# Hybrid RWKV-7 / S5 layer on one core: gelu of the S5 results in fill work, stored in channel order; a tanh behind the sines; the second half's natural layout behind the first half's outputs

## The chip, the cores and the metric

The kernel runs on one core of a Trainium2 chip. Its time is the device time of one execution in microseconds (us), and the time of a kernel is the median over its runs. Next to the times there is one profiled execution, of which a trace shows every instruction of the engines: TensorE (PE, matrix products), VectorE (DVE), ScalarE (ACT), GpSimd (POOL) and SyncE (SP, which here only issues DMA transfers).

## The reference

One decoder layer over 1024 tokens with 1024 channels, fp32. The parts that matter:

```python
h = rms_norm(x, norm_mix_pre)
proj = h @ w_in                      # RWKV inputs | S5 input u (512) | two gates (2 x 1024)
gates = jax.nn.sigmoid(proj[..., N_RWKV_COLS + S5_WIDTH:] + b_gate)
o_rwkv = rwkv7_branch(p_rwkv, ...) @ w_branch_rwkv
# s5_branch: y = Re(C states) + d * u per group of 16 channels, then
y = jax.nn.gelu(y)
o_s5 = (y * jax.nn.sigmoid(y @ w_glu + b_glu)) @ w_branch_s5
mixed = (g_rwkv * o_rwkv + g_s5 * o_s5) @ w_out
x = x + rms_norm(mixed, norm_mix_post)
h = rms_norm(x, norm_ffn_pre)
x = x + rms_norm(conv_ffn(h, ...), norm_ffn_post)
```

`rwkv7_branch` is a recurrence over the tokens with a 64x64 state for each of 8 heads; S5 is a diagonal complex recurrence.

## The kernel before

Every large fp32 product is made of three matmuls on operands split into a high and a low part: L172 (high by high), L173 (low by high) and L174 (high by low). A tile is 128 channels by 512 tokens, so the 1024 tokens are two halves, th = 0 and 1. Matmuls of 512 columns start every 0.227 us at full clock.

The work runs in stages. To about 270 us: input norm, the S5 input projection and the S5 scan in four batches, whose tables come from Sin (L573, L574). Each batch leaves its results in HBM in `YU` (L616), in the scan's layout. Then, for each half, the RWKV stages run as lanes of generators:

- the **front** (`rwkv_front`, for two groups g of two channel tiles u): loads of k, v, r and others from `RKV`, `TZ`, `TA` (L652); Square of k on ACT (L667); Exp (L673, L674); column sums `st` on PE into PSUM buffers `rp` (L681); their inverse roots on DVE and back into `yb` on ACT (L687); transposes `kb` (L701); then the grams (L715, the four-part products inside a chunk);
- the **natural layout** (`rwkv_nat`, L741 for keys, `nat_v` L756 for values): PE transposes that ACT copies out (L748, L750, L761);
- the **inversion** (`rwkv_inv`): a transpose on DVE (L784) of what ACT copies into it (L773), 31 steps of two DVE operations each (L795, L797), a transpose back (L798);
- the **level** (`rwkv_level`): transposes on DVE (L812), small products on PE (L822 and after);
- the **chain** over the chunks (`rwkv_chain`), and the **output** (`rwkv_out`): norm on DVE, PE transposes (L935), ACT evictions (L937), loads of `bv` and `TG` (L944), stores to `YR` (L950).

The chain of half 0 runs at about 392 to 453 us, that of half 1 at about 600 to 700 us.

Beside these lanes lies the **fill** work, a list of generators that yield one small block of matmuls at a time: `gate_tiles` (the 16 tiles of gate projections, evicted by a Tanh on ACT, L1158, and stored to `GT`, L1159), `merge` (`gate` L1203, `glu_tile` L1187, L1188; it loads `YR` at L1210 and the S5 results by `s5_y`), later the output projection. `s5_y` loads a strided piece of `YU` (L1177) and applies gelu on ACT (L1178), which also puts it into channel order. A planner gives each lane's step a latency (T_ numbers, us), and places fill blocks until the step is due; that sets the order of PE, which runs its instructions as written. The other engines' orders follow from a scheduler with priorities. All loads and stores of this region are issued by SP, one after the other: an issue that waits holds the ones behind it.

PSUM buffers: `gm` (products of fill) has two, `rp` two, `cz` two per pair. In SBUF the pool `ld` has ten tiles, the weights' pools four.

Of the kernel before, what the change touches and what calls it, by code (L numbers as in the profile page):

```python
# [66 lines left out]
class Kern:  # L67
# [425 lines left out]
    def s5_tables(self, b, d):  # L493
# [78 lines left out]
        A.activation(cs, ph, AF.Abs)  # L572
        A.activation(sn, ph, AF.Sin, scale=SIN_SCALE)  # L573
        A.activation(cs, cs, AF.Sin, bias=self.hpi, scale=-SIN_SCALE)  # L574
        A.copy(ph, s["rho"][:, g8].unsqueeze(2).to_broadcast([128, 8, 128]))
        G.memset(ph[:, :, 0:1], 0.0)

# [220 lines left out]
            V.transpose(mt.rearrange("p (e t) -> p t e", t=32), x.rearrange("p (q t) -> p t q", t=32))  # L798
            self.diagonal(ds, mt, True)

    def rwkv_level(self, ds):

        A, V = self.nc.scalar, self.nc.vector
        mm = self.nc.tensor.matmul
        lo, hi = (slice(0, 32), slice(64, 96)), (slice(32, 64), slice(96, 128))
        tie = self.rp((128, 8, 64))
        self.nat_v(ds[1], 1, tie)
        Z = [self.tg("ld", NLD).rearrange("p (u c t) -> p u c t", u=2, t=32) for _ in ds]
        for d, xz in zip(ds, Z):
            A.copy(xz[:, :, 0, 0:1], tie[:, 0:2, 0:1])  # L810
            for h in range(2):
                V.transpose(xz[lo[h]].rearrange("p u c t -> p (u c) t"),  # L812
                            d["gr"][lo[h], :, :, h, 0:32].rearrange("p u c t -> p (u c) t"))
        P = [[x.rearrange("p (k c t) -> p k c t", k=2, t=32) for x in y] for y in (self.cz(), (self.rp(), self.rp()))]
        yield 0.4, T_LT
        self.chain_v(ds, 0)
        kw = dict(stop=True, skip_group_check=True)
        for d, p, xz in zip(ds, P, Z):
            for u in range(2):
                for c in range(8):  # L820
                    for h in range(2):
                        mm(p[u][hi[h], 0, c], d["gr"][lo[h], u, c, h, 32:64], xz[lo[h], u, c], start=c == 0, **kw)  # L822
        for p, xz in zip(P, Z):
            for u in range(2):
                for h in range(2):
                    A.copy(xz[hi[h], u], p[u][hi[h], 0])
        yield 1.6, T_LV
        for d, p, xz in zip(ds, P, Z):
            for u in range(2):
                for c in range(8):  # L830
                    for h in range(2):
                        mm(p[u][lo[h], 1, c], xz[hi[h], u, c], d["gr"][hi[h], u, c, h, 32:64], start=c == 0, **kw)
        for d, p in zip(ds, P):
            for u in range(2):
                for h in range(2):
                    A.copy(d["gr"][lo[h], u, :, h, 32:64], p[u][lo[h], 1])
        yield 1.6, T_LV
# [334 lines left out]
    def lx(self):  # L1172
        return self.lxp.tile([128, 512], F32R, tag="lx", name=self.nm("lx"))

    def s5_y(self, t, b, th, y):

        self.nc.sync.dma_start(t, self.YU[b].rearrange("j c g n -> (c g) j n")[:, :, th * 64:th * 64 + 64])  # L1177
        self.nc.scalar.activation(y.rearrange("p (n j) -> p j n", j=8), t, AF.Gelu_apprx_tanh)  # L1178
        return y

    def glu_tile(self, m, xs, t, y, br, to):
# [34 lines left out]
    def merge(self, mg):  # L1216
# [8 lines left out]
            self.split(*br[k], self.yr[k])  # L1225
        xs, ys = [], []

        def inputs(bs):
            for b in bs:
                y = self.hp[0].tile([128, 512], F32, tag=f"hh{4 + b}", name=self.nm("hh"), bufs=1)  # L1230
                ys.append(self.s5_y(self.tg("ld", NLD, (128, 8, 64)), b, 0, y))
                xs.append(self.pair(1, 4 + b))
                self.split(*xs[b], y)
        yield 0
        first = []
        for i in range(NK + MGAP):
# [18 lines left out]
    def s5_inputs(self, b):  # L1255

        assert self.fronts == 4
        self.ys5.append(self.s5_y(self.ev((128, 8, 64)), b, 1, self.tg("ld", NLD)))
        self.xs5.append(self.pair(0, b))
        self.split(*self.xs5[b], self.ys5[b])  # L1260

# [478 lines left out]
    def build(self):  # L1740
        tc, nc = self.tc, self.nc
        with tc.tile_pool(name="const", bufs=1) as self.const, tc.tile_pool(name="small", bufs=1) as self.small, \
# [7 lines left out]

            self.US = [dr(f"US{m}", (8, 16, 8, 128)) for m in range(4)]
            self.YU = [dr(f"YU{m}", (8, 16, 8, 128)) for m in range(4)]
            self.YR = [dr(f"YR{m}", (128, 512)) for m in range(4)]
            self.X1 = dr("X1", (D, T))
            self.H0 = [dr(f"H0{k}", (128, 512)) for k in range(NK)]
# [60 lines left out]
    def front_half(self):  # L1816
# [8 lines left out]
        with tc.tile_pool(name="lxp", bufs=4) as self.lxp, tc.tile_pool(name="s5c", bufs=1) as self.s5c, \  # L1825
# [4 lines left out]
            with tc.tile_pool(name="xp", bufs=1) as xp:  # L1830
                with tc.high_priority(HPN):
                    self.setup(xp)
                    self.s5w = {}
                    self.start(xp)
                    self.setup_vecs()
                with tc.high_priority(HP):
                    self.s5_setup()
                self.fill = [self.mix_in()] + [self.gate_tiles(m) for m in range(14)] + [
                    self.merge_loads(), self.gate_tiles(14, 15)]
                self.outs, self.yr = 0, []  # L1840
            with tc.tile_pool(name="s5p", bufs=1) as self.s5p:
                self.s5d = [{} for _ in range(4)]
# [45 lines left out]
    def chain_lane(self):  # L1888
        for th in range(2):
            ds = self.ds[th]  # L1890
            yield 0, lambda: self.fronts >= 2 * th + 1
            self.rwkv_nat(ds[0], 0)
            yield 2.0, (lambda: self.preps > th), 2.5
            yield from self.rwkv_level(ds)
            yield 0, lambda: self.outs >= 2 * th
            yield from self.rwkv_chain(ds, self.pts[th], th)
            if th:
# [17 lines left out]


T_US, T_TAB0, T_TAB, T_TRIG, T_SCAN = 5.0, 44.0, 20.0, 12.0, 24.0
T_LD, T_SQ, T_LT = 6.0, 3.0, 3.5
NEVA = 4
T_KN, T_BK, T_GR, T_NF, T_MT, T_INV, T_LV, T_CH = 7.0, 4.0, 4.0, 5.0, 3.0, 34.0, 1.0, 0.8  # L1920
T_LN, T_LE, T_INV2 = 32.0, 16.0, 46.0
# [4 lines left out]
NLD = 10  # L1926
# [80 lines left out]
```

## Time and profile before

| what | value |
|---|---|
| median of 3 runs | 1463.06 us (1462.29 to 1465.25) |
| profiled execution, its own time | 1461.26 us |
| its span | 1459.5 us |
| mean granted TensorE clock | 0.986 |

A row of the timeline gives start and duration in us, engine, line and operation, output and input by name, and in brackets how long the engine had been idle and what ended it. A row of the waits gives who waited for whom: us in total, times, longest. A row of the windows gives the busy time (and number of instructions) of PE, PE's weight loads, DVE, ACT and POOL, the granted TensorE clock, the busy share of the DMA engines and GB/s. An arrow as in `ld<-YU` reads "ld is written from YU".

### The profile page before, as it was taken

The page shows a single profiled execution, that of the slowest core. Times are in us where ns is not written, and L with a number is a line of the kernel's source. Part 1 is how long each engine was busy: PE and PEld are TensorE (multiplying, and loading weights), DVE is VectorE, ACT ScalarE, POOL GpSimd, SP SyncE. Part 2 cuts the span into 40 slices and gives each one's busy share as a digit, 9 for nine tenths or more (in the row PEclk, how much of TensorE's full clock was granted, in tenths as well). Part 3 has the DMA queues.
Part 4 walks back from the last instruction along what each step waited for, and adds up shares of the span by engine and source line. Part 5 has one row for each costly group of instructions (what it writes and reads, how often), then busy time and mean ns, then how long its engine had stood idle before and what let it go on. Part 6 is the DMA issues. An engine that isn't in the chain of part 4 may idle for free. (4 is left out here: it accounts for less than half of the span.)

```text
span 1459.5 us, 23887 instructions
## 1 busy us (share of the span) xinstructions
PE 1402.2 (96%) x9156; PEld 1142.9 (78%) x9156; DVE 1087.5 (75%) x1783; ACT 746.7 (51%) x1197; POOL 34.9 (2%) x80
## 2 busy tenths in 40 slices
PE   7999999999999989899999999999999999999996
PEld 5778888878878767678788887888888887888785
DVE  8986886378327788548688898777777777597677
ACT  7667775453424564535455464454544445444451
POOL 0000000000000000000000000000000000000001
PEclk9999999999999999899999999999999999999998
DMA  7454433542413565433555543222222228934723
GB/s 221 116 190 128 144 117 108 188 146 80 139 60 110 162 193 165 138 111 116 172 195 180 158 133 122 87 83 76 75 84 87 87 73 273 328 112 144 239 79 115
DMA packets 119682, 202.04 MB, mean 138 GB/s; under 512 B 28672, under 2 KB 34944, under 8 KB 119568
## 3 DMA queue, kind: packets, MB, share of 16 engines
q1 hardware_dynamic: 113296, 182.43, 39.4%
q0 software_dynamic: 4544, 15.80, 2.9%
q10 hardware_dynamic: 1728, 2.29, 0.4%
q8 instruction: 72, 1.18, 0.3%
q14 instruction: 42, 0.34, 0.1%
HBM read 148.04 MB, written 50.33 MB: 136 GB/s over the span
## 5 line engine op out<-in xcount | busy, mean ns | idle before, releaser
L172 PE MATMUL gm<-hh,wh 128*128 128x512 f32 x672 | 276.2, 411 | 9.1 <-DVE hl L1203 4.6
L173 PE MATMUL gm<-hl,wh 128*128 128x512 f32 x672 | 264.8, 394 | 0.0
L174 PE MATMUL gm<-hh,wl 128*128 128x512 f32 x672 | 264.6, 394 | 0.0
L156 ACT CAST wh<-wf 128x512 fp32r<-128x512 f32 x171 | 105.2, 618 | 140.9 <-PE gm L173 72.5
L157 DVE TENSOR_TENSOR wl<-wf,wh 128x512 fp32r<-128x512 f32 x171 | 117.2, 688 | 76.2 <-ACT wh L156 75.6
L172 PEld LDWEIGHTS gm<-hh,wh 128*128 128x128 f32 x672 | 127.5, 190 | 41.5 <-DVE hl L1203 5.7
L174 PEld LDWEIGHTS gm<-hh,wl 128*128 128x128 f32 x672 | 127.7, 190 | 27.8
L173 PEld LDWEIGHTS gm<-hl,wh 128*128 128x128 f32 x672 | 127.8, 190 | 24.7 <-issue 1.0
L1626 PE MATMUL d<-xl,wh 128*128 128x512 f32 x308 | 120.7, 392 | 2.1 <-DVE xl L227 2.0
L1625 PE MATMUL d<-xh,wh 128*128 128x512 f32 x308 | 120.8, 392 | 2.1 <-ACT xh L226 2.1
L1627 PE MATMUL d<-xh,wl 128*128 128x512 f32 x308 | 120.6, 392 | 0.0
L1451 PE MATMUL rp<-t,h 128*128 128x512 f32 x216 | 84.4, 391 | 1.5 <-ACT p L1465 1.5
L1453 PE MATMUL rp<-t,l 128*128 128x512 f32 x216 | 84.2, 390 | 0.5 <-DVE l L227 0.5
L1452 PE MATMUL rp<-t,h 128*128 128x512 f32 x216 | 84.1, 389 | 0.0
L1626 PEld LDWEIGHTS d<-xl,wh 128*128 128x128 f32 x308 | 58.2, 189 | 15.5 <-DVE xl L227 3.4
L1625 PEld LDWEIGHTS d<-xh,wh 128*128 128x128 f32 x308 | 58.2, 189 | 14.6 <-ACT xh L226 2.4
L1627 PEld LDWEIGHTS d<-xh,wl 128*128 128x128 f32 x308 | 58.1, 189 | 12.0
L226 ACT CAST h<-r 128x1024 fp32r<-128x1024 f32 x34 | 35.8, 1054 | 61.1 <-PE rp L1452 29.6
L227 DVE TENSOR_TENSOR l<-r,h 128x1024 fp32r<-128x1024 f32 x34 | 41.6, 1225 | 29.2 <-ACT h L226 27.7
L1472 DVE SCALAR_TENSOR_TENSOR y<-zv,vecs,y 128x1023 f32<-128x1023 f32 (+1 forms) x36 | 46.1, 1281 | 8.5 <-ACT y L1470 8.5
L1465 ACT COPY p<-rp 128x512 f32<-128x512 f32 x54 | 31.0, 574 | 36.6 <-PE rp L1453 36.6
L1451 PEld LDWEIGHTS rp<-t,h 128*128 128x128 f32 x216 | 40.5, 188 | 11.1 <-ACT p L1465 2.4
(459 smaller groups left out, 3127.6 us busy)
## 6 DMA issues: line engine op xcount, KB each, us to landing
r<-in_w_up_dram SPq DMA_DIRECT2D x36, 512.0 KB, 3.6
wf<-in_w_in_dram SPq DMA_DIRECT2D x62, 256.0 KB, 3.0
st<-in_w_down_dram SPq DMA_DIRECT2D x55, 256.0 KB, 4.0
st<-ACT SPq DMA_DIRECT2D x44, 256.0 KB, 4.3
wf<-in_w_up_dram SPq DMA_DIRECT2D x36, 256.0 KB, 2.9
ACT<-y POOLq DMA_DIRECT2D x18, 512.0 KB, 2.9
GT<-ev SPq DMA_DIRECT2D x32, 256.0 KB, 2.5
wf<-in_w_br_dram SPq DMA_DIRECT2D x32, 256.0 KB, 2.6
```

What stands on the lines that cost most here:

```text
L156: nc.scalar.copy(h[:, :n], f[:, :n])
L157: nc.vector.tensor_tensor(l[:, :n], f[:, :n], h[:, :n].bitcast(F32), ALU.subtract)
L172: mm(ps, a, xh[k], start=k == 0, stop=False)
L173: mm(ps, a, xl[k], start=False, stop=False)
L174: mm(ps, b, xh[k], start=False, stop=k == n - 1)
L1451: mm(ps, wh[:, c], xh, start=first and k == 0, stop=False, skip_group_check=True)
L1452: mm(ps, wh[:, c], xl, start=False, stop=False, skip_group_check=True)
L1453: mm(ps, wl[:, c], xh, start=False, stop=k == 3, skip_group_check=True)
L1472: V.scalar_tensor_tensor(y[:, lag:], z[:, 0:1024 - lag], self.vec(nme, i), y[:, lag:], ALU.mult, ALU.add)
L1625: mm(ps, wh[:, c], xh[:, x], start=start, stop=False, skip_group_check=True)
L1626: mm(ps, wh[:, c], xl[:, x], start=False, stop=False, skip_group_check=True)
L1627: mm(ps, wl[:, c], xh[:, x], start=False, stop=stop, skip_group_check=True)
```

## The change

Four edits. (a) `s5_tables` of the last batch ends with a Tanh of one column, so that ACT's table is changed behind the last Sin and not at the first gate tile. (b) A new piece of fill work, `s5_ready`, loads a piece of `YU`, applies gelu and stores it to new tensors `Y5` in HBM in channel order; eight of them stand behind the gate tiles 6 to 13. `s5_y` is then one contiguous load of `Y5`. `merge` issues its four loads at its start, into the tiles `hh4` to `hh7`. (c) `chain_lane` places the natural layout of the second half behind the outputs of the first. (d) The latency of the level is 6.0 instead of 3.5 us for the second half, which puts nine more fill matmuls in front of its products.

```diff
@@ s5_tables
         A.activation(cs, cs, AF.Sin, bias=self.hpi, scale=-SIN_SCALE)
+        if b == 3:
+            A.activation(self.edge[:, 0:1], cs[:, 0, 0:1], AF.Tanh)
@@ rwkv_level
-    def rwkv_level(self, ds):
+    def rwkv_level(self, ds, latency):
...
-        yield 0.4, T_LT
+        yield 0.4, latency
@@ s5_y
-    def s5_y(self, t, b, th, y):
-
+    def s5_ready(self, b, th):
+
+        t, y = self.tg("ld", NLD, (128, 8, 64)), self.tg("ld", NLD)
         self.nc.sync.dma_start(t, self.YU[b].rearrange("j c g n -> (c g) j n")[:, :, th * 64:th * 64 + 64])
         self.nc.scalar.activation(y.rearrange("p (n j) -> p j n", j=8), t, AF.Gelu_apprx_tanh)
+        self.nc.sync.dma_start(self.Y5[b][:, th * 512:th * 512 + 512], y)
+        yield 0
+
+    def s5_y(self, b, th, y):
+
+        self.nc.sync.dma_start(y, self.Y5[b][:, th * 512:th * 512 + 512])
         return y
@@ merge
+        for b in range(4):
+            y = self.hp[0].tile([128, 512], F32, tag=f"hh{4 + b}", name=self.nm("hh"), bufs=1)
+            ys.append(self.s5_y(b, 0, y))
+
         def inputs(bs):
             for b in bs:
-                y = self.hp[0].tile([128, 512], F32, tag=f"hh{4 + b}", name=self.nm("hh"), bufs=1)
-                ys.append(self.s5_y(self.tg("ld", NLD, (128, 8, 64)), b, 0, y))
                 xs.append(self.pair(1, 4 + b))
-                self.split(*xs[b], y)
+                self.split(*xs[b], ys[b])
@@ s5_inputs
-        self.ys5.append(self.s5_y(self.ev((128, 8, 64)), b, 1, self.tg("ld", NLD)))
+        self.ys5.append(self.s5_y(b, 1, self.tg("ld", NLD)))
@@ the tensors in HBM
+            self.Y5 = [dr(f"Y5{m}") for m in range(4)]
@@ the list of fill work
-                self.fill = [self.mix_in()] + [self.gate_tiles(m) for m in range(14)] + [
-                    self.merge_loads(), self.gate_tiles(14, 15)]
+                self.fill = [self.mix_in()] + [self.gate_tiles(m) for m in range(6)]
+                for i in range(8):
+                    self.fill += [self.gate_tiles(6 + i), self.s5_ready(i % 4, i // 4)]
+                self.fill += [self.merge_loads(), self.gate_tiles(14, 15)]
@@ chain_lane
-            yield 0, lambda: self.fronts >= 2 * th + 1
+            yield 0, lambda: self.fronts >= 2 * th + 1 and self.outs >= 2 * th
             self.rwkv_nat(ds[0], 0)
             yield 2.0, (lambda: self.preps > th), 2.5
-            yield from self.rwkv_level(ds)
+            yield from self.rwkv_level(ds, T_LT2 if th else T_LT)
@@ the planner's numbers
-T_LD, T_SQ, T_LT = 6.0, 3.0, 3.5
+T_LD, T_SQ, T_LT, T_LT2 = 6.0, 3.0, 3.5, 6.0
```

On ACT, the front of the second half's group 1 stood like this (L667 the Squares of k, `wh` a weight's high part, L1158 a gate tile's eviction):

```order
L1158 ACTIVATE ev_5267<-gm_5185,hb_b_gate 128x512
L667 ACTIVATE gr_5246<-ld_5249,vecs 128x512
L667 ACTIVATE gr_5246<-ld_5251,vecs 128x512
L156 CAST wh_5372<-wf_5374 128x512
L673 ACTIVATE gr_5246<-ld_5253 128x8x64
```

and now, with the lines of the changed file (the Squares are L669, the gate's eviction L1160, the gelu L1181, and L689 puts the inverse roots into `yb`, formerly L687):

```order
L1181 ACT_TABLE_LOAD
L1181 ACTIVATE ld_5088<-ld_5087 128x8x64
L1181 ACTIVATE ld_5209<-ld_5208 128x8x64
L156 CAST wh_5423<-wf_5425 128x512
L1160 ACTIVATE ev_5397<-gm_5310,hb_b_gate 128x512
L669 ACTIVATE gr_5286<-ld_5289,vecs 128x512
L689 ACTIVATE gr_5286<-sv_5446 128x512
L669 ACTIVATE gr_5286<-ld_5291,vecs 128x512
```

A table load and two gelus came ahead of the gate's eviction and the Squares, and the second Square now stands behind the first L689.

A little later ACT had, before, the two L687, the copies of the natural layout and the eviction L937 of the first output tile (rows between are left out at the dots):

```order
L687 ACTIVATE gr_5246<-sv_5401 128x512
L687 ACTIVATE gr_5246<-sv_5405 128x512
L748 COPY bk_845_4896<-cz_5430 128x4x64
L750 COPY bk_845_4896<-cz_5430 64x4x64 x2
L761 COPY V_847_4898<-rp_5434 64x4x64 x4
...
L937 ACTIVATE ld_5494<-rp_5489,vecs 128x512
L1158 ACTIVATE ev_5509<-gm_5384,hb_b_gate 128x512
L937 ACTIVATE ld_5540<-rp_5535,vecs 128x512
```

and now (Exp is L675 and L676, the outputs' eviction L939):

```order
L677 ACTIVATE bk_918_5285<-ld_5299,ka_785,ka_h 128x8x64
L676 ACTIVATE ld_5295<-ld_5295 128x512
L698 COPY pt_2897<-gr_5286 128x8 x2
L1181 ACT_TABLE_LOAD
L1181 ACTIVATE ld_5401<-ld_5400 128x8x64
L939 ACTIVATE ld_5486<-rp_5481,vecs 128x512
L939 ACTIVATE ld_5506<-rp_5501,vecs 128x512
L939 ACTIVATE ld_5530<-rp_5525,vecs 128x512
```

The natural layout's copies have gone further back, and a table load with the last gelu stands directly ahead of the first output's eviction.

On SP, before, the loads of v (`RKV_99`, `RKV_100`) and k (`RKV_97`, `RKV_98`) of the same front stood together:

```order
L652 DMA ld_5165<-RKV_99 128x512
L652 DMA ld_5168<-RKV_100 128x512
L652 DMA ld_5249<-RKV_97 128x512
L652 DMA ld_5251<-RKV_98 128x512
L652 DMA ld_5253<-TZ_65 128x512
```

and now:

```order
L1161 DMA GT_88<-ev_5307 128x512
L1180 DMA ld_5087<-YU_108 128x8x64
L155 DMA wf_6038<-in_w_br_dram 128x512
L654 DMA ld_5200<-RKV_99 128x512
L654 DMA ld_5203<-RKV_100 128x512
L1180 DMA ld_5208<-YU_109 128x8x64
L1182 DMA Y_112<-ld_5088 128x512
L654 DMA ld_5289<-RKV_97 128x512
L1182 DMA Y_113<-ld_5209 128x512
...
L1161 DMA GT_89<-ev_5518 128x512
L1180 DMA ld_5400<-YU_110 128x8x64
L946 DMA ld_5488<-bv_2902 128x512
L1182 DMA Y_114<-ld_5401 128x512
```

The loads of k stand behind the stores `Y_112` and `Y_113`, which wait for their gelus, and the last load of `YU` behind the store of a gate tile, `GT_89`.

On PE, from the second `st` (L681, now L683) to the outputs' transposes (L935, now L937), before:

```order
L681 MATMUL rp_5396<-csts,gr_5246 128x2 x4
L172 MATMUL gm_5384<-hh_612,wh_5360 128x512
L173 MATMUL gm_5384<-hl_613,wh_5360 128x512
L174 MATMUL gm_5384<-hh_612,wl_5361 128x512
L741 MATMUL cz_5430<-csts,bk_845_4896 128x128 x4
...
L174 MATMUL gm_5384<-hh_669,wl_5367 128x512
L935 MATMUL rp_5489<-csts,mt_4200 128x128 x4
L172 MATMUL gm_5384<-hh_686,wh_5366 128x512
...
```

and now:

```order
L683 MATMUL rp_5441<-csts,gr_5286 128x2 x4
L172 MATMUL gm_5429<-hh_616,wh_5405 128x512
...
L937 MATMUL rp_5501<-csts,mt_4215 128x128 x4
L172 MATMUL gm_5429<-hh_730,wh_5411 128x512
L173 MATMUL gm_5429<-hl_731,wh_5411 128x512
L174 MATMUL gm_5429<-hh_730,wl_5412 128x512
L172 MATMUL gm_5521<-hh_565,wh_5417 128x512
L173 MATMUL gm_5521<-hl_566,wh_5417 128x512
L174 MATMUL gm_5521<-hh_565,wl_5418 128x512
L937 MATMUL rp_5525<-csts,mt_4215 128x128 x4
...
```

The natural layout (L741, L756) has gone from behind `st` to behind the four output tiles, which now stand before it; the third output's transposes, `rp_5525`, come three matmuls behind the last one of the gate tile `gm_5429`, and take the `rp` buffer that the first output, `rp_5481`, had.

## The prediction

> **What bounds the kernel now.** I read first the page's busy times, then TensorE's waits in the stretches that the edits touch, then each engine's timeline there.
>
> ```profile
> PE 1402.2 (96%) x9156; PEld 1142.9 (78%) x9156; DVE 1087.5 (75%) x1783; ACT 746.7 (51%) x1197; POOL 34.9 (2%) x80
> ```
>
> PE is busy 96% of the span, so an edit can only win what PE waits, plus what its clock loses behind a wait. All edits work between 198 us and 604 us. There PE waits once at 269 us and then in the second half's front and merge.
>
> ```profile
> 269.15 0.50 PE L172 MATMUL gm<-hh,wh 128*128 128x512 f32 x1 [1.05 <-ACT ev L1158]
> 481.21 1.92 PE L681 MATMUL rp<-csts,gr 128*128 128x2 f32 x16 [0.28 <-DVE ld L730]
> 495.21 0.66 PE L701 MATMUL rp<-csts,gr 128*128 128x128 f32 x4 [2.03 <-ACT ld L937]
> 533.21 0.50 PE L172 MATMUL gm<-hh,wh 128*128 128x512 f32 x1 [3.90 <-DVE hl L1203]
> PE gm L172 <- DVE hl L1203: 4.6, 2, 3.9
> PE gm L172 <- DVE ev L1203: 3.1, 2, 2.2
> PE rp L822 <- DVE ld L812: 3.0, 1, 3.0
> PE cz L822 <- ACT hh L231: 2.2, 1, 2.2
> PE rp L756 <- DVE ld L730: 1.7, 1, 1.7
> PE cz L822 <- DVE ld L812: 0.4, 1, 0.4
> ```
>
> The first four rows are the timeline's, the others the waits between 500 and 600 us, which add up to 15.0 us. Most name DVE. So from about 518 us PE keeps pace with DVE, which runs the inversion, the merge's evictions and the level's transposes in one order:
>
> ```profile
> 518.32 2.26 DVE L784 STREAM_TRANSPOSE mt<-mt 128x1024 f32<-128x1024 f32 x1
> 532.48 0.68 DVE L1203 SCALAR_TENSOR_TENSOR hl<-ev,gm 128x512 f32<-128x512 f32 x1
> 596.77 0.70 DVE L812 STREAM_TRANSPOSE ld<-gr 32x512 f32<-32x512 f32 x1
> 532.48:597.47 64.99, 54.73 (x322) 43.39 (x322) 57.42 (x114) 36.45 (x68) 0.00 (x0) 0.91 0.52 158
> ```
>
> The inversion's first transpose starts at 518.32, the first gate is evicted at 532.48, and the level's last transpose ends at 597.47. Over the last 65 us DVE is busy 57.4 us, 88%; 7.6 us are idle. What the changed order puts on DVE before 597 us, and how late the inversion starts, decides the time.
>
> **Edit (a), the Tanh behind the sines.** Now the table is loaded at the first gate tile:
>
> ```profile
> 267.11 1.28 ACT L1158 ACT_TABLE_LOAD   x1
> ```
>
> PE's wait of 1.05 us at 269.15 is behind it. At its new place ACT has idle time around 198 us and PE no wait for it. Gain 1.05 us. The gelus i = 0 to 4 of edit (b) lie beside the first chain, where ACT is half idle; one of them delays a copy of the chain by 0.9 us against 0.8 us that PE has in hand. Cost 0.1, taken as 0.2, at most the 1.15 us of a gelu. Sum −0.85.
>
> **Edit (b) in the second front.** ACT, SP and the transfers are priced by these rows: the duration of a table load and a gelu, the Squares, the store behind which the loads queue, and the landing times (least, median, most) of `YU`, `RKV`, `TG` and `YR` in that order.
>
> ```profile
> 520.34 1.28 ACT L1178 ACT_TABLE_LOAD   x1
> L1178 ACT ACTIVATE hh<-ld 128x512 f32<-128x512 f32 x4 | 4.7, 1164 | 1.3 <-DMA ld<-YU 1.3
> 470.88 1.32 ACT L667 ACTIVATE gr<-ld,vecs 128x512 f32<-128x512 f32 x2
> 463.67 1.86 SPq L652 DMA_DIRECT2D ld<-RKV  x4
> DMA to landing us min/median/max: 2.6/3.5/6.2
> DMA to landing us min/median/max: 2.0/3.5/5.4
> DMA to landing us min/median/max: 2.1/3.4/5.0
> DMA to landing us min/median/max: 2.0/4.3/5.1
> ```
>
> The loads of k, issued within 1.86 us from 463.67, now stand behind the store `Y_112` of a gelu. ACT reaches that gelu behind the two squares of the first half's norm, which the new DVE order lets start at about 473 (an estimate). Then come those squares 1.15, a weight's half 0.62, the table 1.28 and the gelu 1.16: 477.2; with two issues the first k lands at 477.6 + 3.5 = 481.1, and its Square ends at 481.8, when PE has reached the first `st` at 480.9. With the longest landing it is 2.9 us late, so I take 2.0 (1.0 to 2.9). The second `st` waits for the first's roots on DVE, L689 and the second Square, which follow each other now: 0.48 + 0.34 + 0.62 + 0.66 = 2.1. Both replace the 0.28 at 481.21: **+3.8** (3.0 to 4.7).
>
> **Edits (b) and (c) at the outputs.** The third output's transposes stand three matmuls (0.68 us) behind the gate tile `gm_5429`. They need the first output's PSUM buffer, whose eviction stands on ACT behind the last gelu, whose load stands on SP behind that gate tile's store:
>
> ```profile
> L1158 ACT ACTIVATE ev<-gm,hb_b_gate 128x512 f32<-128x512 f32 x5 | 3.4, 685 | 4.1 <-PE gm L174 4.1
> L937 ACT ACTIVATE ld<-rp,vecs 128x512 f32<-128x512 f32 x4 | 3.1, 778 | 2.4 <-PE rp L935 2.3
> 471.01 0.32 SPq L1159 DMA_DIRECT2D GT<-ev  x1
> ```
>
> Eviction 0.69 and 0.05 for the hand-over, the store's issue 0.33, landing 3.5, table 1.28 (it holds the wait for the load in this order), gelu 1.0 until its result can be passed, eviction 0.78, less 0.68: **6.9 us** (6.0 with the shortest landing, 9.7 with the longest), in place of the 2.03 at 495.21: +4.9. A wait of that length costs clock too: after the 3.90 at 533.21 the next matmuls were 0.43 apart in place of 0.227, and the window shows 0.83:
>
> ```profile
> 534.25 0.63 PE L173 MATMUL gm<-hl,wh 128*128 128x512 f32 x1
> 534.68 0.63 PE L174 MATMUL gm<-hh,wl 128*128 128x512 f32 x1
> 530.00:540.00 10.00, 6.79 (x23) 5.49 (x24) 7.33 (x17) 8.14 (x20) 0.00 (x0) 0.83 0.48 154
> ```
>
> That is 0.17 of 10 us, 1.7 us; I put it into the upper end only. On the other side the natural layout ran at that rate behind the wait at 481.21: six groups from 484.39 to 487.9, 3.5 us.
>
> ```profile
> 484.39 1.91 PE L741 MATMUL cz<-csts,bk 128*128 128x128 f32 x8
> 487.57 0.60 PE L756 MATMUL rp<-csts,ld 128*128 128x128 f32 x4
> ```
>
> The last of them, at full clock, took 0.36 until the next matmul began; six such are 2.1, so in its new place it saves 1.4.
>
> The Trainium skill, "ScalarE: Activation LUTs", section "What ACT_TABLE_LOAD costs", puts every change of set at about 2.66 us, 1.28 of load and 1.38 of drain, and asks for calls to be grouped by set; that speaks against this edit, which goes from 8 table loads in all to 12. By its price the sum would be 1.38 higher at each of the two loads above. Here the load at 520.34 begins 0.03 us behind the end of the instruction before it, and the gelu starts 1.29 after the load began, so the trace shows no drain:
>
> ```profile
> 521.63 1.15 ACT L1178 ACTIVATE hh<-ld 128x512 f32<-128x512 f32 x1
> ```
>
> The fourth output waits 1.5 us (0.7 to 2.5) for a PSUM buffer that DVE releases late, and the values' second transposes wait 1.3 (ACT copies of 0.37 each and L773 stand ahead). The first gram stood here:
>
> ```profile
> 500.82 1.98 PE L715 MATMUL cz<-ar,bk 64*64 64x128 f32 x64
> ```
>
> Twelve matmuls and the fourth output's transposes now stand ahead of it, so for the same work it stood at 500.82 + 12 × 0.227 + 0.35 = 503.9, and PE is now 3.8 + 4.9 + 1.5 + 1.3 − 1.4 = **10.1 us late**, at 514.0.
>
> **What this makes of the stage that DVE paces.** SP cannot issue the four `Y5` loads into `hh4` to `hh7` until gate tile `gm_5521` has ended, at 512.3 (nine matmuls before the gram); the fourth output's `bv`, `TG`, its store and its `YR` load queue behind. And ACT has put the copies for the inversion behind the split of that `YR`. Before, this took
>
> ```profile
> 509.41 0.41 SPq L944 DMA_DIRECT2D ld<-TG  x1
> 519.69 0.62 ACT L226 CAST hh<-ld 128x512 fp32r<-128x512 f32 x1 [0.31 <-DMA ld<-YR]
> L773 ACT COPY mt<-gr 32x512 f32<-32x512 f32 x4 | 2.5, 618 | 0.6 <-PE rp L935 0.5
> ```
>
> 10.9 us from the `TG` issue to the end of the split. With 2.0 for the issues ahead and 1.4 for two copies that is 14.3, and about 3 for the rows of SP that now stand between: 17.4 (14.3 to 20.4). The inversion starts at 529.7, 11.4 late. In the new order 18 DVE rows in place of 28 stand from there to the first gate's eviction (four inversion steps at 0.65 and two low parts at 0.69 went behind it): 14.2 − 2.6 − 1.4 = 10.2, so 539.9, 7.4 late. From it to the level's last transpose come 122 rows where there were 110, 57.4 + 4.0 = 61.4 us of work. As DVE is now the late one, I take 97% busy: 63.3 in place of 65.0. The level's last transpose ends 5.7 late; nine matmuls (2.05 us) are done that came after it. With −0.85: **+2.8**. The ends: 88% busy as before makes 69.8 and +9.3; landings at their least take 0.9 (`YU` twice), 1.5, 1.3 and 2.3 off the chain, 6.9 in all, and make −4.1. After the level, work and order are as before, with the same fill.
>
> **The rivals.**
> - *A, faster: the loads are quick.* All new chains hang on landings. At their least the sum is 2.8 − 6.9 = −4.1: 1459.0. For it: the least are in the rows; against: the medians are 3.4 to 4.3, and the DMA engines are 88% busy where the last of them go, by this row's last share:
>
> ```profile
> 518.32:532.48 14.16, 9.34 (x51) 7.49 (x49) 12.72 (x31) 12.43 (x20) 1.08 (x2) 1.00 0.88 254
> ```
>
> - *B, faster: DVE has time.* The inversion's result is wanted 21 us after it ends,
>
> ```profile
> 568.58 1.70 DVE L773 COPY gr<-mt 32x512 f32<-32x512 f32 x4
> 591.18 1.43 DVE L812 STREAM_TRANSPOSE ld<-gr 32x512 f32<-32x512 f32 x2
> ```
>
> so lateness of 11.4 might be swallowed, and the 15.0 us of waits go: 10.1 − 0.85 − 15.0 = −5.7, 1457.4. Against: these 21 us are filled with evictions that PE waits for.
> - *C, slower: DVE's idle time stays.* DVE's 7.6 us of idle are waits for PE, which are not shortened by being late, and PE's waits cost clock again. From the point where DVE stays under 90% busy after its late start, the sum is +8.1 to +9.3: 1471.5.
> - *D: the waits trade places.* The change does what it says, removed and new waits cancel and only (a) is left: −0.9, 1462.2.
> - *E, slower: a change of table costs more than its load.* Two of the new loads lie on chains of PE; a drain of 1.38 each gives 2.8 + 2.8 = +5.6, 1468.7. The rows at 520.34 speak against it. (By the Trainium skill's page named above.)
>
> **How the numbers follow.** The sum is made against the profiled execution, 1461.26 us: 1464.1. The median of the runs is 1.8 higher, 1463.06, so I predict 1465.8. What a measurement of this kernel can tell from no change is 0.2%, 2.9 us: 1460.1 to 1466.0. The forecast, from 1463 to 1469, gets 0.42, of which 0.25 lie within the bound and 0.17 above. A gets 0.17 (0.13 faster, 0.04 within), B 0.11 faster, C 0.16 slower, D 0.08 within, E 0.06 slower. So faster 0.24, same 0.37, slower 0.39. The range 1457.5 to 1472 reaches from B to C and leaves out the tails of both.
>
> **What would show it.** In the new trace: no wait at 269; the `st` of the second half's group 1 waits 3 to 5 us; one wait of 6 to 7 us of PE at the third output for the eviction L939, with half-rate matmuls behind it; inversion's transpose L786 near 529; the first gate L1212 at 540; the level's last L814 near 603, with DVE 97% busy before. If PE's long wait at the output isn't there, or L786 starts before 525, rivals A or B hold; if DVE is under 90% busy from 540 to 603, C. I am wrong altogether if waits of more than 2 us appear in the first half's chain (392 to 453 us) or after 604.

## The result, and the profile after

The changed kernel takes 1486.09 us in the median of 6 runs (1479.10 to 1489.33), the kernel before 1462.67 (1458.34 to 1465.25). The ratio is 1.0159 with a 95% interval of 1.0128 to 1.0190: slower by 23 us. The forecast was 1465.8, and the range ended at 1472.

The profiled execution has a span of 1487.2 us against 1459.5, 27.7 more. The first page line splits this: PE has the same 9156 instructions and is 10.1 us longer busy, since more of them ran at half clock (the mean granted clock is 0.978 against 0.986; at 0.5, matmuls of 512 columns start 0.43 us apart in place of 0.227), and 17.6 us longer idle.

```profile
PE 1412.3 (95%) x9156; PEld 1150.7 (77%) x9156; DVE 1087.7 (73%) x1783; ACT 751.4 (51%) x1202; POOL 34.9 (2%) x80
```

PE's longest waits between 390 and 760 us of the changed kernel (us in total, times, longest):

```profile
PE rp L937 <- ACT ld L939: 9.7, 1, 9.7
PE rp L683 <- ACT gr L669: 5.8, 2, 4.1
PE gm L172 <- DVE ev L1212: 5.8, 1, 5.8
PE cz L881 <- DVE S L906: 4.6, 1, 4.6
PE gm L172 <- ACT ev L1160: 3.1, 1, 3.1
PE gm L172 <- DVE hl L1212: 1.8, 2, 1.0
PE rp L758 <- ACT V L763: 1.4, 1, 1.4
PE gm L172 <- ACT hh L226: 1.2, 1, 1.2
PE rp L824 <- DVE ld L814: 1.0, 1, 1.0
```

Of the old waits, the 5.6 us at the level have fallen to 1.0, and the 1.7 us at the values' transposes have become 1.4. New are the third output (9.7), the two `st` (5.8) and, in the first chain, a wait for the state S (4.6). The last is where the prediction expected none: a wait of over 2 us in this chain is what it had named as the sign of being wrong altogether. The wait of 3.1 us for the eviction of a gate tile (L1160) is new too; e1 and e10 below, which have edit (c) and no early gelus, show it with 4.0 us each.

How late PE is can be read by counting its instructions, which are the same in both kernels up to the second half's front: 2.6 us at the first chain's start (395.2 against 392.6; 1.5 of it is there at 81 us already, ahead of every edit, and one stretch of half clock more came at 312), 11.1 at that chain's last product (458.3 against 447.2), 14.9 at `st` (496.06 against 481.21), and 27.7 at the end.

**The first chain.** First SP, then DVE and PE of the changed kernel:

```profile
392.35 0.32 SPq L1182 DMA_DIRECT2D Y<-ld  x1
...
396.45 0.32 SPq L1182 DMA_DIRECT2D Y<-ld  x1
...
399.55 0.96 SPq L654 DMA_DIRECT2D ld<-TZ  x2
...
404.89 2.34 DVE L673 TENSOR_TENSOR_SCAN ld<-csts,ld 128x512 f32<-128x512 f32 x2 [5.25 <-DMA ld<-TZ]
407.15 0.40 DVE L905 TENSOR_TENSOR S<-S,cz 128x256 f32<-128x256 f32 x1
408.06 1.14 PE L881 MATMUL cz<-S,ar 64*64 64x64 f32 x32 [4.61 <-DVE S L906]
```

and the kernel before:

```profile
382.32 0.92 SPq L652 DMA_DIRECT2D ld<-TZ  x2
386.69 2.34 DVE L671 TENSOR_TENSOR_SCAN ld<-csts,ld 128x512 f32<-128x512 f32 x2 [1.76 <-DMA ld<-TZ]
```

The two scans over `tz` belong to the second half's front, which nobody wants yet. DVE has them, in its fixed order, ahead of the chain's first update of S. Before, `tz` was loaded at 382.3 and the scans were done before the chain began. Now its loads stand behind the stores to `Y5`, which wait for gelus 3 and 4 (counted from 0), and behind the weight's load and the gate tile's store that follow these, and were issued at 399.6. So DVE stood still for 5.25 us, and the chain waited 4.61 us for it. Half clock came on top: 0.83 over these 20 us, where the chain of before had 1.00.

```profile
400.00:420.00 20.00, 15.39 (x228) 11.30 (x226) 5.04 (x8) 3.52 (x8) 0.00 (x0) 0.83 0.34 112
```

**`st` and the third output.** ACT, then SP of the changed kernel between 485 and 519 us, and three of SP's waits from 480 to 515 (the longest, 16.4 us in two, are for the evictions of gate tiles whose stores come next):

```profile
485.08 0.60 ACT L156 CAST wh<-wf 128x512 fp32r<-128x512 f32 x1
485.70 1.28 ACT L1181 ACT_TABLE_LOAD   x1
486.99 1.16 ACT L1181 ACTIVATE ld<-ld 128x512 f32<-128x512 f32 x1
493.27 1.12 ACT L1181 ACTIVATE ld<-ld 128x512 f32<-128x512 f32 x1 [5.12 <-DMA ld<-YU]
...
495.29 0.71 ACT L669 ACTIVATE gr<-ld,vecs 128x512 f32<-128x512 f32 x1
...
509.02 0.69 ACT L1160 ACTIVATE ev<-gm,hb_b_gate 128x512 f32<-128x512 f32 x1 [3.39 <-PE gm L174]
...
516.39 1.28 ACT L1181 ACT_TABLE_LOAD   x1 [4.75 <-DMA ld<-YU]
517.68 1.12 ACT L1181 ACTIVATE ld<-ld 128x512 f32<-128x512 f32 x1
518.60 1.40 ACT L939 ACTIVATE ld<-rp,vecs 128x512 f32<-128x512 f32 x2
...
486.81 0.33 SPq L155 DMA_DIRECT2D wf<-in_w_br_dram  x1
...
488.14 0.43 SPq L1180 DMA_DIRECT2D ld<-YU  x1
...
509.73 0.32 SPq L1161 DMA_DIRECT2D GT<-ev  x1
513.51 0.37 SPq L1180 DMA_DIRECT2D ld<-YU  x1
```

```profile
SPq L1182 <- ACT ld L1181: 4.2, 1, 4.2
SPq L155 <- DVE rsh L138: 4.2, 1, 4.2
SPq L1180 <- DVE ld L696: 3.4, 1, 3.4
```

Gelu 6 waits 5.12 us for a load that SP issued at 488.14, behind a weight load for which SP had waited 4.2 us for DVE, and that took 5.1 us to land, where the median of the eight is 3.1. The Squares (L669) stand behind that gelu. But the k of the first Square, issued at 489.74 behind the store of gelu 5, took 4.7 us and landed at 494.4, so that gelu 6 makes at most 0.9 us of the wait for this Square (495.29). The k of the second was issued at 494.78, behind the store of gelu 6, which had held SP for another 4.2 us, and landed at 498.6; its Square began at 498.73.

The last gelu shows a link that the prediction left out: SP had stored the gate tile at 509.73 and was free, but issued the load of `YU` at 513.51, after a wait of 3.4 us for DVE's L696. L696 is a reader of tiles of `ld`, and the load goes into one of the ten tiles of `ld`. L696 itself is late, since it comes behind the `st` and what ACT makes of them, which the gelus had put off: the new loads wait for work that waits for them.

On the change of table: the load at 485.70 ends at 486.98 and the gelu starts at 486.99, and the weight's cast ahead of it had ended at 485.68. By the Trainium skill, "ScalarE: Activation LUTs", section "What ACT_TABLE_LOAD costs", some 1.38 us of drain belong to a change of set; these rows again show none.

**The stage that DVE paces.** The copies L775 for the inversion stand on ACT behind the split of the last `YR` load, as predicted. The inversion starts at 554.36 (predicted 529.7), the first gate is evicted at 563.08 (539.9), and the level's last transpose ends at 630.6 (603):

```profile
552.45 0.62 ACT L226 CAST hh<-ld 128x512 fp32r<-128x512 f32 x1 [5.21 <-DMA ld<-YR]
554.36 2.08 DVE L786 STREAM_TRANSPOSE mt<-mt 128x1024 f32<-128x1024 f32 x1 [0.58 <-ACT mt L775]
563.08 0.69 DVE L1212 SCALAR_TENSOR_TENSOR hl<-ev,gm 128x512 f32<-128x512 f32 x1
629.88 0.70 DVE L814 STREAM_TRANSPOSE ld<-gr 32x512 f32<-32x512 f32 x1
563.08:630.60 67.52, 58.94 (x350) 47.03 (x348) 61.23 (x127) 32.65 (x65) 0.18 (x1) 0.95 0.50 158
```

DVE's work in the stretch is 61.2 us, as predicted (61.4), but it is busy 91% of it and not 97%. Between 540 and 603 us it is busy 56.1 of 63 us, 89%, which is the sign that the prediction had named for rival C (under 90%).

### The profile page after: what moved, and what is told of

The parts are those of the page before. It is cut to its first block, busy times and chain, and to the rows that moved or that the text cites. A ratio compares the mean times of both kernels' runs of the same rounds, so it can differ in the third digit from the quotient of the medians.

```text
span 1487.2 us, 23935 instructions
## 1 busy us (share of the span) xinstructions
PE 1412.3 (95%) x9156; PEld 1150.7 (77%) x9156; DVE 1087.7 (73%) x1783; ACT 751.4 (51%) x1202; POOL 34.9 (2%) x80
## 5 line engine op out<-in xcount | busy, mean ns | idle before, releaser
L174 PEld LDWEIGHTS gm<-hh,wl 128*128 128x128 f32 x672 | 128.9, 192 | 28.3
L226 ACT CAST h<-r 128x1024 fp32r<-128x1024 f32 x34 | 35.8, 1054 | 61.1 <-PE rp L1463 29.6
L227 DVE TENSOR_TENSOR l<-r,h 128x1024 fp32r<-128x1024 f32 x34 | 41.6, 1224 | 29.2 <-ACT h L226 27.7
```

Source lines behind the costliest of these rows:

```text
L174: mm(ps, b, xh[k], start=False, stop=k == n - 1)
L227: (eng or self.nc.vector).tensor_tensor(lo, x, hi.bitcast(F32), ALU.subtract)
```

## The experiments

Theory 1: the early gelus make the loss; their loads and stores stand in SP's order and take tiles of `ld`, so the second half's loads and everything behind the gelus on ACT come late. Rival 2: the natural layout's new place makes it. Rival 3: the changes of table cost it. All ratios are against the kernel before, run beside them on the same chip.

| run | what it is | median us | ratio (95%) |
|---|---|---|---|
| the change | all four edits | 1486.09 | 1.0159 (1.0128 to 1.0190) |
| e1_no_early_gelu | without edit (b) | 1466.33 | 1.0023 (1.0008 to 1.0037) |
| e2_early_gelu_alone | edit (b) alone | 1479.68 | 1.0120 (1.0088 to 1.0151) |
| e10_nat_behind_alone | edit (c) alone | 1471.94 | 1.0051 (1.0032 to 1.0071) |
| e11_level_alone | edit (d) alone | 1461.04 | 0.9979 (0.9957 to 1.0001) |
| e12_tanh_and_level | (a) and (d) | 1457.00 | 0.9963 (0.9947 to 0.9979) |
| e14_level_nine | as e12, latency 9.0 | 1460.15 | 0.9976 (0.9964 to 0.9988) |
| e3_store_pool | all, stores by GpSimd | 1477.73 | 1.0109 (1.0065 to 1.0154) |
| e4_all_pool | all, loads and stores by GpSimd | 1476.03 | 1.0095 (1.0067 to 1.0122) |
| e15_load_in_ev | all, gelu's input from `ev` | 1471.45 | 1.0069 (1.0044 to 1.0095) |
| e16_ev_and_pool | e4 and e15 together | 1469.38 | 1.0030 (1.0011 to 1.0050) |
| e13_last_late | all, last gelu late | 1479.38 | 1.0104 (1.0078 to 1.0130) |
| e8_three_late | all, gelus 5 to 7 late | 1471.69 | 1.0068 (1.0047 to 1.0090) |
| e9_late_gelus | all, gelus 4 to 7 late | 1473.90 | 1.0066 (1.0034 to 1.0099) |
| e7_gelu_earlier | all, gelus early | 1470.55 | 1.0060 (1.0040 to 1.0080) |

### Which edit

**e1_no_early_gelu**: the changed kernel with `s5_ready`, `Y5` and the new `s5_y` taken back.

> The changed kernel without the early gelus: S5 results pass gelu in the merge as before; the Tanh behind the sines, the natural layout behind the outputs and the level latency of 6.0 us stay. Theory 1 (the early gelus with their loads and stores hold the second half's loads back, by the SP queue or by the tiles of the pool ld): the three waits of the changed kernel (4.6 us in the first chain for S, 4.1 and 1.8 us at st, 9.7 us at the third output) are gone, and the time is 1455 to 1466. Rival 2 (the natural layout behind the outputs makes the waits): the wait at the third output stays above 5 us and the time is above 1472.

It came 0.3 us above the upper end, and the three waits went as follows: S none, `st` 0.3 us (for a PSUM buffer), the third output 3.2. So the early gelus make about 1.36% of the 1.59%. But what is left is not faster than before either. Of the 3.2 us at the third output, 2.3 are a tile of `ld` again: the first output's eviction writes into one and waits on ACT for the same L696.

**e2_early_gelu_alone**: edits (a), (c) and (d) taken back.

> The kernel before with the early gelus alone, without the Tanh behind the sines, with the natural layout and the level as before. Theory 1: all three waits are there (over 3 us in the first chain for S, 5 to 6 us at the two st, over 5 us at the third output or at the transposes kb that follow st), and the time is 1480 to 1495. Rival 2: the time is 1458 to 1468.

S waits 5.4 us, `st` 5.9, and a wait of 5.2 us stands at the outputs, now for the values' copies. 1.20% alone and 1.36% on top of the others: within these intervals the early gelus cost the same with the natural layout in either place. The median is 0.3 us under the expected range.

**e10_nat_behind_alone**, with one line changed in the kernel before, and **e11_level_alone**:

```diff
-            yield 0, lambda: self.fronts >= 2 * th + 1
+            yield 0, lambda: self.fronts >= 2 * th + 1 and self.outs >= 2 * th
```

```diff
-            yield from self.rwkv_level(ds)
+            yield from self.rwkv_level(ds, T_LT2 if th else T_LT)
```

> The kernel before with the natural layout of the second half behind the outputs, alone (level latency 3.5 us, gelus in the merge, no Tanh behind the sines). Theory 1 (the new place trades the waits at 495 and 524 us for others at the outputs and behind them): waits between 470 and 610 us in sum within 3 us of those before, time 1461 to 1468. Rival (the new place gains and the longer level latency takes it back): 1455 to 1460.

> The kernel before with the level latency of 6.0 us for the second half alone. Theory 1 (nine fill matmuls more cover waits for the level's transposes): PE's waits for the level (5.6 us before) fall to 2 to 4 us, nothing else moves, time 1459 to 1463. Rival (it costs): 1464 or more.

Edit (c) costs more than either side expected: 1471.94, the waits between 470 and 610 us add up to 22.1 us against 17.5 before (4.6 more, where theory 1 allowed 3), and a wait of 6.4 us appears at the level. Edit (d) behaves as theory 1 has it: 5.6 us of waits for the level fall to 2.6, and the time is 0.2% lower, with an interval that just reaches 1.

**e12_tanh_and_level** has (a) and (d) without (b) and (c), **e14_level_nine** has a latency of 9.0 in place of 6.0.

> The kernel before with the Tanh behind the sines and the level latency of 6.0 us, without the early gelus and with the natural layout in its old place. Theory 1: the level's waits 2 to 3 us lower, the wait at the first gate tile 0.8 in place of 1.05; time 2 to 3 us under the kernel before, 1459 to 1461.5. Rival: no difference from it, 1462 to 1464.

> As the run with the Tanh and the level latency of 6.0, with a latency of 9.0 us, which puts fifteen matmuls (3.4 us) more in front of the level's second products. Theory 1 (the level's waits are covered as far as fill stands there): PE's waits for the level fall to under 0.5 us, the time is 1 to 3 us lower, 1457 to 1460. Rival (the wait only moves behind the level, since DVE sets the pace): within 1 us of the run with 6.0.

e12 has the lowest median, under both kernels: 0.9963 (0.9947 to 0.9979), 2 us more of a gain than expected. Its wait at the first gate tile is 0.78 us, so the Tanh brings 0.27 us by this row and not 1.05; with the 3.0 us that went at the level this makes 3.3 of some 5 us, and where the rest comes from is not shown. With the latency of 9.0 the level's wait falls to 0.5 us, but the gates wait more (12.2 us for L1205 where e12 has 7.9), and the time does not fall further: 1460.15 against 1457.00. Its mechanism is the rival's, its time lies above the bands of both.

e1 and e12 differ in edit (c) alone, and both reach `st` at 484 us. What (c) does shows in PE's timeline behind it, first e12, then e1 (L743 is the natural layout, L717 the grams, L937 the outputs; rows before and between are left out):

```profile
505.24 1.98 PE L717 MATMUL cz<-ar,bk 64*64 64x128 f32 x64
508.63 0.60 PE L937 MATMUL rp<-csts,mt 128*128 128x128 f32 x4
511.91 1.98 PE L717 MATMUL cz<-ar,bk 64*64 64x128 f32 x64
```

```profile
505.29 1.04 PE L743 MATMUL cz<-csts,bk 128*128 128x128 f32 x8
506.60 1.04 PE L743 MATMUL cz<-csts,bk 128*128 128x128 f32 x8
513.71 1.98 PE L717 MATMUL cz<-ar,bk 64*64 64x128 f32 x64
519.96 1.98 PE L717 MATMUL cz<-ar,bk 64*64 64x128 f32 x64
```

In e12 the natural layout comes right behind `st`, at 486.57, and the fourth output behind the first gram. In e1 the natural layout stands behind all four outputs, and the fourth output and twelve fill matmuls more stand ahead of the grams, which come 8.5 and 8.1 us later. The added work itself is 3.1 us (12 × 0.227 and 0.35). The rest are waits, 5.6 us in e1 from the second `st` to the first gram against 3.3 in e12, and the clock: the window 486.1 to 513.7 of e1 was granted 0.81, which loses 5.2 us, the window 485.7 to 505.2 of e12 0.91, which loses 1.8. On the grams waits the inversion:

```profile
518.33 1.25 ACT L775 COPY mt<-gr 32x512 f32<-32x512 f32 x2 [0.34 <-DVE gr L721]
```

```profile
528.17 1.24 ACT L775 COPY mt<-gr 32x512 f32<-32x512 f32 x2 [4.09 <-DVE gr L721]
```

In e12 it is ready at 518.3 and in e1 9.8 us later. The level ends 11.0 us later (609.9 against 598.9), and 2.7 us of that come back as the 12 fill matmuls (0.227 each) that were done earlier; the span differs by 6.6 us. Part of what remains is again the clock behind the level: from 598 to 607 e12 was granted 0.62, from 609 to 618 e1 0.81, which is 1.7 us less lost.

### What holds the gelus and what they hold

**e3_store_pool**, **e4_all_pool**, **e15_load_in_ev** and **e16_ev_and_pool** keep every gelu in its place among the fill work:

```diff
-        self.nc.sync.dma_start(self.Y5[b][:, th * 512:th * 512 + 512], y)
+        self.nc.gpsimd.dma_start(self.Y5[b][:, th * 512:th * 512 + 512], y)
```

(e3; e4 does the same to the load of `YU`), and

```diff
-        t, y = self.tg("ld", NLD, (128, 8, 64)), self.tg("ld", NLD)
+        t, y = self.ev((128, 8, 64)), self.tg("ld", NLD)
```

(e15; e16 is e4 with this line).

> The changed kernel with the stores to Y5 issued by GpSimd in place of SyncE; loads stay on SyncE. Theory 1a (SP's order holds the loads: a load waits behind a store that waits for a gelu): the wait for S in the first chain and the waits at st shrink to under 1 and under 2 us, the one at the third output stays (its load stands behind a gate tile's store), and the time falls by 6 to 12 us to 1474 to 1481. Theory 1b (the ten tiles of ld hold the loads): waits within 1 us of those of the changed kernel, 1482 to 1490.

> The changed kernel with the loads of YU and the stores of Y5 both issued by GpSimd. Theory 1c (what is left of the early gelus' price after the stores have left SyncE is that their loads wait in SyncE's order, so that gelus and what stands behind them on ScalarE start late): the waits at st fall from 5.2 us with the stores alone moved to under 2, the third output to under 5, and the time is 4 to 8 us under that run, 1470 to 1474. Rival (the gelus' own place on ScalarE and the pool ld hold it): st still waits 4 us or more, the time is within 3 us of that run.

> The changed kernel with the early gelus' input tile taken from the pool ev (three tiles, used by gate tiles) in place of ld (ten tiles, used by the RWKV loads); issues stay on SyncE. Theory 1d (the tiles of ld are the shared resource: the load of YU cannot be issued until a tile of ld comes free, and then the gelu, the Squares and the output's eviction behind it on ScalarE start late): the third output waits under 4 us in place of 9.7, the two st under 3 us in sum, the time falls to 1470 to 1477. Rival (the gelus' place on ScalarE and in SyncE's order is enough): the third output still waits over 7 us, 1481 or more.

> The same with the loads of YU and the stores of Y5 issued by GpSimd. Theory 1d and 1a together (tiles of ld, and SyncE's order): what is left over the run without early gelus (1466.3) is under 5 us, 1466 to 1471, the third output under 4 us and st under 2 us. Rival (the gelus and table loads on ScalarE themselves cost the rest): 1473 or more.

e3: the wait for S fell to 1.4 us (expected under 1) and the time by 0.5%, into the band of theory 1a, though the interval just overlaps that of the change; the third output fell too, to 6.9, but `st` still waited 5.2 (expected under 2). SP's order is a part of it, not all. e4: `st` fell to 2.4, which the rival had excluded, but the third output rose to 10.8, and the time is within 2 us of e3's: the rival's number. The wait for S was 2.9.

Here is GpSimd's last load of `YU` in e4:

```profile
503.37 0.91 POOL L1180 DMA_DIRECT2D ld<-YU  x1 [14.85 <-DVE ld L696]
```

GpSimd had nothing else to do, and waited for the same DVE instruction as SP in the changed kernel. So it is the tile of `ld` that holds this load, on either queue.

e15 takes the input tile elsewhere: the third output waits 5.3 us (expected under 4), the two `st` 2.4, and the ratio falls from 1.0159 to 1.0069. The wait for S is gone, but the loads of `tz` are issued at 433.8 there, DVE's scans wait 6.33 us for them, and the chain waits 3.5 us for U at 442.8 instead: the same link at another chunk. SP's order changes with it (the last `YU` load now stands ahead of the gate tile's store), so e15 alone does not separate tile and order; with the two rows on L696 it does for the last gelu.

The gelu's output tile is still one of `ld`: in e15 the last gelu itself waits 1.06 us for L696, in e16 0.9. e16, with neither the input tile in `ld` nor the transfers on SP, keeps 1.0030 against 1.0023 without early gelus: their intervals overlap, though it still waits 4.4 us for L939, where 4 was the bound, and 1.8 for U. What gelus and table loads on ACT cost as such is then at most some tenths of a per cent; rival 3 does not carry the loss.

### Where the gelus stand

**e13_last_late**, **e8_three_late** and **e9_late_gelus** place the last one, three or four of the early gelus behind the last gate tile; **e7_gelu_earlier** places all eight behind the gate tiles 0 to 7. For e8:

```diff
-                    self.fill += [self.gate_tiles(6 + i), self.s5_ready(i % 4, i // 4)]
+                    self.fill += [self.gate_tiles(6 + i)] + ([self.s5_ready(i % 4, i // 4)] if i < 5 else [])
                 self.fill += [self.merge_loads(), self.gate_tiles(14, 15)]
+                self.fill += [self.s5_ready(i, 1) for i in range(1, 4)]
```

> The changed kernel with the last early gelu alone behind the last gate tile. Theory 1 (the last gelu alone makes the 9.7 us at the third output; gelus 5 and 6 make those at st): st still waits 5 to 6 us, the third output under 5, the time is 6 to 10 us under the changed kernel's, 1476 to 1480. Rival (PE being late changes what the outputs wait for; one gelu does not matter): the third output still waits over 7 us, 1482 to 1488.

> The changed kernel with the early gelus 5, 6 and 7 moved behind the last gate tile, so that they pass ScalarE after the first half's outputs; 0 to 4 stay. Theory 1 (gelus 5 and 6 ahead of the Squares on ScalarE make the waits at st, and the seventh makes the one at the third output): st waits under 1 us, the third output under 4 us, the wait for S in the first chain stays at 4 to 6 us; the time is 16 us under the changed kernel's, 1466 to 1474. Rival (both waits come from the natural layout's new place or from DVE): the wait at the third output stays above 6 us and the time above 1478.

> The same with gelu 4 moved back too, so that the loads of tz for the second half's front are issued before the first chain wants DVE. Theory 1: the wait for S in the first chain is under 1 us, and the time is 4 to 7 us under that of the run with three late gelus, 1461 to 1468. Rival (the wait for S comes from ScalarE being busy with gelus 0 to 3): the wait for S stays above 3 us and the two runs are within 2 us.

> The changed kernel with the eight early gelus behind the gate tiles 0 to 7 in place of 6 to 13, so that all are done before the second half's front begins. Table loads stay 12. Theory 1: no wait over 2 us at st, at the third output or for S in the first chain; time 1455 to 1466. Rival 3 (the changes of the table on ScalarE cost, each 2.7 us, wherever they stand): 1468 or more.

e13 came as theory 1 says: `st` 5.9 us, the third output 4.7, 1479.38; its interval just overlaps that of the change. e8 too in its time, the waits at `st` are gone, and S waits 3.1 (4 to 6 expected); the third output still waits 4.7 us, but for DVE:

```profile
PE gm L173 <- DVE hl L227: 4.8, 2, 2.9
PE rp L937 <- DVE mt L930: 4.7, 1, 4.7
PE gm L172 <- ACT hh L226: 4.1, 1, 4.1
```

That is edit (c) again: PE comes to the outputs before their norm (L930) is done. And the merge's splits wait for the late gelus (L227, L226).

e9: the wait for S is gone, as expected, but the time is no lower than e8's. A wait of 1.8 us for U in the chain (`tz` is issued at 393.5, still later than the 382.3 of before) and 7.9 us at the splits take the place. This expectation failed, and the wait for S is shown to hang on gelu 4, but what it costs in the end was not shown by this pair.

e7: `st` has no wait, the third output 4.7 us for L930. The time is 4.2 us over e1's, above the range of theory 1 and inside that of rival 3 (1468 or more): this expectation failed too. PE waits 3.9 us for `kb`'s result L705 in the *first* half's front, where e1 has 1.0: the early gelus there push back other loads. As many table loads cost e16 next to nothing, which speaks for the place and against their number, but no run tried that place without them, so this is argued and not shown.

## Why the prediction was wrong

Its sum was 25 us short, and 24.7 of them are there when the inversion starts: the early gelus beside the first chain, taken as 0.2 us; `st`, the outputs and the half clock behind each wait; and the way from the grams to the inversion. Behind that two misses cancel: the stretch from the inversion to the level's end made up 2.9 us where 5.7 were forecast, and 2.7 us of fill that had been done in the meantime were not counted. By its own steps:

- *Edit (a), gain 1.05.* The wait became 0.8. The table load that ended at 268.39 hid behind the gate tile's own products, which were complete only about then; what PE waits for is the eviction of 0.69 itself. The size was wrong by 0.8. (The table is now loaded at 237.12 and not around 198; nothing waits for it there either.)
- *The gelus i = 0 to 4 "lie beside the first chain, where ACT is half idle", cost 0.1.* **Wrong.** I looked at ACT, where the gelus run, and not at SP, where their stores stand ahead of the loads of `tz`, nor at DVE's order, where the scans on `tz` stand ahead of the chain's S. Measured: 4.6 us of wait and half clock behind it, so that PE went from 2.6 us late to 11.1.
- *`st`, +3.8.* The mechanism was right; the waits are 4.06 and 1.77 against 0.28, +5.6, and with the half clock PE lost 7.1 us (11.1 late before, 18.2 at the end of the second `st`) where 3.8 were forecast. The term counted gelu 5 and its store. The store's issue took 1.02 us and the first k 4.7 to land in place of 3.5; the second k stood behind the store of gelu 6, whose own load was late. (The term's lower end, given as 3.0, is 2.8 by its own terms.)
- *The third output, 6.9.* Right in its links but one: 3.4 of the 9.7 us are the tile of `ld` that DVE's L696 frees. I priced the issue at 0.33 us from a row whose queue was free, and did not ask what the load's target was waiting for. The 3.4 us are all that the term was short of, and a little over: without them it would have been 6.3.
- *At the first gram PE is "10.1 us late".* **Wrong.** It was 31.1 late: 535.0 against 503.9. Of this 11.1 are the first chain's and what lies ahead of it, 7.1 were lost at `st` (3.8 forecast), and 12.9 from there to the gram (6.3 forecast). Edit (c)'s own share, which I took as 1.5 + 1.3 − 1.4 us beside the 3.1 us of work that the order puts ahead of the gram, showed alone in e10 and e1: 8.5 us in place of 4.5. The work was counted rightly; the half clock behind each new wait was not in the sum, and the waits were longer.
- *From the gram to the inversion.* 15.7 us were forecast, 19.4 measured, by the links that were named. With the 21 us before it the inversion starts 24.7 us behind the forecast.
- *DVE's stage at 97% busy.* It was 91%, between the forecast and rival C (88%), and C's sign showed. But the lateness came from ahead of it: the inversion starts 36.0 us late and the level's last transpose ends 33.1 late, so this stretch still took less time than before.
- *The fill that comes back.* The forecast took off nine matmuls (2.05 us). By the level's last transpose 21 more are done than before, the nine of edit (d) and the twelve that edit (c) put ahead of the grams, 4.8 us: 33.1 becomes 28.3. Here the forecast was 2.7 us too high.
- *After the level* the forecast holds: no new wait above 1 us, and from the first product of the up-projection (917.2 against 888.8) to the end PE stays 28 us late.

The one term for half clock, 1.7 us, was kept for "the upper end only". By the busy time of PE some 10 of the span's 27.7 us are of this kind, and 1.5 us were there ahead of every edit.

That the time went up was in the forecast. But nearly a third of the loss came from a step priced at 0.2 us, so the right sign is in part luck.

## What to carry to other kernels

A load or store that is added to an in-order queue costs what stands behind it, not its own 0.4 us: list, for each added issue that waits, the next issues on that queue and the first instruction on any engine that stands behind their data in a fixed order. Ask of each added tile who freed it: a small ring shared by two streams of work ties the one to the other, whatever queue issues the transfer. And when a piece of work is moved behind another, price what then stands behind both (here the grams and the inversion), the waits of each piece that changed its neighbours, and the clock behind every new wait.

## What the hardware showed that I had not expected

Half clock is not tied to long waits alone. In the kernel before it came after 0.28 us of idle time and sixteen products with two columns (matmuls 0.43 us apart in place of 0.227):

```profile
483.54 0.63 PE L173 MATMUL gm<-hl,wh 128*128 128x512 f32 x1
483.97 0.63 PE L174 MATMUL gm<-hh,wl 128*128 128x512 f32 x1
```

The same products with the same short wait do not bring it each time: in e12, after 0.27 us at 484.01, the next matmuls stand 0.23 us apart:

```profile
486.11 0.40 PE L173 MATMUL gm<-hl,wh 128*128 128x512 f32 x1
486.34 0.39 PE L174 MATMUL gm<-hh,wl 128*128 128x512 f32 x1
```

Waits of 2 to 3 us are not alike either: behind the 2.03 us at 495 of the kernel before, the window 495 to 500 was granted 1.00, and behind 2.60 us in e12 the window 499 to 503 was granted 0.57. What decides is not shown here, so a forecast does well to carry half clock behind each new wait as a range.

In the changed kernel, the window that holds `st` and the third output was granted 0.72:

```profile
490.00:520.00 30.00, 14.46 (x57) 11.74 (x56) 17.73 (x34) 13.97 (x21) 1.08 (x2) 0.72 0.54 169
```

In the two traces compared here, transfers of `YU` issued by GpSimd took longer than by SP; least, median and most from issue to landing, first in the changed kernel, then in e4:

```profile
DMA to landing us min/median/max: 2.8/3.1/5.1
```

```profile
DMA to landing us min/median/max: 3.7/4.3/6.4
```
